# Rotary embedding: the early store of two rows replaced by an early write of 512 bytes of zeros per partition

## The chip, the cores and the metric

The kernel runs on one core of a Trainium2 chip. The metric is the device time in microseconds (us); lower is better. The kernel before took 317.1 us (median of 3 runs, 317.05 to 317.19).

A ratio below is the mean time of one kernel's runs over the mean of the other's runs of the same rounds, so it is not quite the ratio of the medians quoted beside it.

Some words first. HBM is the chip's large memory, SBUF the memory on the core, of 128 partitions. POOL (GpSimd), DVE (VectorE), ScalarE (ACT in the profile) and SyncE (SP) are engines of the core. POOL, ScalarE and SyncE each issue transfers to a queue of their own, and the same 16 DMA engines do the work of all queues. A transfer is a DMA; the trace has a record for each of its rows, called a packet here. When a DMA engine has done its part, it adds one to a counter, which is the completion increment, and also has a record; the DMA has landed when all 16 have come. An operation is gated by, or held behind, a DMA when it may start only after that has landed.

## The reference

`x` has shape (8, 2048, 16, 64) in float32. Each row of 64 is a pair of halves, rotated by an angle that depends on the position:

```python
x1, x2 = x[..., :32], x[..., 32:]
out1 = x1 * cos - x2 * sin
out2 = x1 * sin + x2 * cos
return np.concatenate([out1, out2], axis=-1)
```

67.1 MB are read and 67.1 MB written; there is little arithmetic.

## The kernel before

A batch is one tile: 128 partitions, each with 16 positions of 16 x 64 numbers, 64 KB in float32 in HBM and 32 KB in float16 in SBUF. The POOL queue loads with a cast to float16 and stores with a cast back. DVE does three operations per batch. There are five buffers, so five loads are issued at once, and later loads wait for stores to free a buffer.

The first two positions of batch 0 (`JA = 2`, 1 MB in all) go another way: they are loaded in float32 on the SyncE queue, worked on first, and written back on the SyncE queue by an early store, which is held behind load 3. In the code below, and in every diff, `...` marks what is left out.

```python
    def store(b, xt):
        j0 = JA if b == 0 else 0                 # batch 0: 14 of 16 positions
        nc.gpsimd.dma_start(out=..., in_=xt[:, j0:J, :, :]...)
    # ... rotate(xt, j0, j1): two multiplications and an addition on DVE ...
    tiles = [load(b) for b in range(NBUF)]       # NBUF = 5, POOL queue
    # ... ScalarE casts: head -> tiles[0], sin, -sin, cos ...
    rotate(tiles[0], 0, JA)
    nc.scalar.copy(out=head..., in_=tiles[0][:, 0:JA, :, :]...)
    early = nc.sync.dma_start(out=out[0]...[:, 0:JA, :]..., in_=head...)
    tc.add_manual_dep(early.ins, loads[3].ins.name, ...,
                      reason="the first rows go out behind this load")
    for b in range(B):
        rotate(tiles[b], JA if b == 0 else 0, J)
        if b < B - 1:
            store(b, tiles[b])
        if b + NBUF < B:
            tiles.append(load(b + NBUF))
    # ... the last batch goes out in three parts ...
```

Of the kernel before, what the change touches and what calls it, by code (L numbers as in the profile page):

```python
# [1 line left out]

# [4 lines left out]


@with_exitstack  # L10
def kernel(
    ctx: ExitStack,
    tc: tile.TileContext,
    x: bass.AP,
    cos: bass.AP,
    sin: bass.AP,
    out: bass.AP,
):
    nc = tc.nc
    f16 = mybir.dt.float16  # L20
    f32 = mybir.dt.float32

    B, S, H, D = x.shape
    Dh = D // 2
    P = nc.NUM_PARTITIONS
    J = S // P
    NBUF = 5

    const_pool = ctx.enter_context(tc.tile_pool(name="rope_const", bufs=1))
    io_pool = ctx.enter_context(tc.tile_pool(name="rope_io", bufs=NBUF))  # L30
    tmp_pool = ctx.enter_context(tc.tile_pool(name="rope_tmp", bufs=1))

    JA = 2
    head = const_pool.tile([P, JA, H, D], f32)
    x0 = x[0].rearrange("(p j) h d -> p j (h d)", j=J)
    nc.sync.dma_start(  # L36
        out=head.rearrange("p j h d -> p (j h d)"),
        in_=x0[:, 0:JA, :].rearrange("p j f -> p (j f)"),
    )
    sin_f = const_pool.tile([P, J, Dh], f32)  # L40
    cos_f = const_pool.tile([P, J, Dh], f32)
    cos_h = const_pool.tile([P, J, Dh], f16)
    sin_h = const_pool.tile([P, J, D], f16)
    nc.sync.dma_start(out=sin_f, in_=sin.rearrange("(p j) d -> p j d", j=J))  # L44
    nc.sync.dma_start(out=cos_f, in_=cos.rearrange("(p j) d -> p j d", j=J))

    loads = []

    def load(b):
        xt = io_pool.tile([P, J, H, D], f16)  # L50
        j0 = JA if b == 0 else 0
        dma = nc.gpsimd.dma_start(  # L52
            out=xt[:, j0:J, :, :].rearrange("p j h d -> p (j h d)"),
            in_=x[b].rearrange("(p j) h d -> p j (h d)", j=J)[:, j0:J, :].rearrange("p j f -> p (j f)"),
        )
        loads.append(dma)
        return xt

    def store(b, xt):
        j0 = JA if b == 0 else 0  # L60
        nc.gpsimd.dma_start(  # L61
            out=out[b].rearrange("(p j) h d -> p j (h d)", j=J)[:, j0:J, :].rearrange("p j f -> p (j f)"),
            in_=xt[:, j0:J, :, :].rearrange("p j h d -> p (j h d)"),
        )

    def rotate(xt, j0, j1):
        v = tmp_pool.tile([P, J, H, D], f16)
        n = j1 - j0
        js = slice(j0, j1)
        shape = [P, n, H, 2, Dh]  # L70
        sin_b = sin_h[:, js, :].rearrange("p j (e d) -> p j e d", e=2).unsqueeze(2).to_broadcast(shape)
        cos_b = cos_h[:, js, :].unsqueeze(2).to_broadcast([P, n, 2 * H, Dh])
        xe = xt[:, js, :, :].rearrange("p j h (e d) -> p j h e d", e=2)
        nc.vector.tensor_mul(  # L74
            out=v[:, js, :, :].rearrange("p j h (e d) -> p j h e d", e=2),
            in0=xe[:, :, :, ::-1, :],
            in1=sin_b,
        )
        xw = xt[:, js, :, :].rearrange("p j h (e d) -> p j (h e) d", d=Dh)
        nc.vector.tensor_mul(out=xw, in0=xw, in1=cos_b)  # L80
        xa = xt[:, js, :, :].rearrange("p j h d -> p (j h d)")
        nc.vector.tensor_add(out=xa, in0=xa, in1=v[:, js, :, :].rearrange("p j h d -> p (j h d)"))  # L82

    tiles = [load(b) for b in range(NBUF)]
    nc.scalar.copy(  # L85
        out=tiles[0][:, 0:JA, :, :].rearrange("p j h d -> p (j h d)"),
        in_=head.rearrange("p j h d -> p (j h d)"),
    )
    nc.scalar.copy(out=sin_h[:, :, Dh:D], in_=sin_f)  # L89
    nc.scalar.mul(out=sin_h[:, :, 0:Dh], in_=sin_f, mul=-1.0)  # L90
    nc.scalar.copy(out=cos_h, in_=cos_f)  # L91
    rotate(tiles[0], 0, JA)
    nc.scalar.copy(  # L93
        out=head.rearrange("p j h d -> p (j h d)"),
        in_=tiles[0][:, 0:JA, :, :].rearrange("p j h d -> p (j h d)"),
    )
    early = nc.sync.dma_start(
        out=out[0].rearrange("(p j) h d -> p j (h d)", j=J)[:, 0:JA, :].rearrange("p j f -> p (j f)"),
        in_=head.rearrange("p j h d -> p (j h d)"),
    )  # L100
    tc.add_manual_dep(
        early.ins,
        loads[3].ins.name,
        mybir.DependencyInfo(mybir.DependencyClass.Sync, mybir.DependencyReason.DATA),
        reason="the first rows go out behind this load",
    )
    def part(b, j0, j1):
        return (
            out[b].rearrange("(p j) h d -> p j (h d)", j=J)[:, j0:j1, :].rearrange("p j f -> p (j f)"),
            tiles[b][:, j0:j1, :, :].rearrange("p j h d -> p (j h d)"),  # L110
        )

    for b in range(B):
        rotate(tiles[b], JA if b == 0 else 0, J)
        if b < B - 1:
            store(b, tiles[b])
        if b + NBUF < B:
            tiles.append(load(b + NBUF))
    dst, src = part(B - 1, 0, 9)
    gate = nc.gpsimd.dma_start(out=dst, in_=src)  # L120
    dst, src = part(B - 1, 9, J - JA)
    rest = nc.gpsimd.dma_start(out=dst, in_=src)  # L122
    tc.add_manual_dep(
        rest.ins,
        gate.ins.name,
        mybir.DependencyInfo(mybir.DependencyClass.NoSync, mybir.DependencyReason.DATA),
        reason="order of the ring",
    )
    dst, src = part(B - 1, J - JA, J)
    nc.scalar.copy(out=head.rearrange("p j h d -> p (j h d)"), in_=src)  # L130
    end = nc.sync.dma_start(out=dst, in_=head.rearrange("p j h d -> p (j h d)"))
    tc.add_manual_dep(
        end.ins,
        gate.ins.name,
        mybir.DependencyInfo(mybir.DependencyClass.Sync, mybir.DependencyReason.DATA),
        reason="the last rows go out behind this part",
    )


# [1 line left out]
_INS = ['x', 'cos', 'sin']  # L141
_OUTS = [((8, 2048, 16, 64), 'float32')]


# [23 lines left out]
```

## Time and profile before

The first lines to read are those of the page: busy time, the DMA row in 40 slices (tenths of the 16 engines' time), the queues and the HBM traffic.

```profile
span 315.4 us, 127 instructions
...
DVE 209.1 (66%) x27; ACT 8.7 (3%) x7; POOL 9.4 (3%) x21
...
DMA  9899999999998989999999999999999999999998
...
q0 software_dynamic: 2448, 98.04, 97.2%
q1 hardware_dynamic: 720, 3.67, 7.7%
HBM read 67.63 MB, written 67.11 MB: 427 GB/s over the span
```

The DMA row never falls below 8: the DMA engines are the limit, and DVE at 66% is not. The two shares of the queues add up to over 100%: a few packet records are very long without moving data.

The second view is the timeline. Its columns are start, length, engine, line, operation, output and input, and in brackets how long the engine sat idle and what ended that. The length of a DMA line is only its issue.

```profile
34.09 1.23 DVE L80 TENSOR_TENSOR xt<-xt,cos_h 128x2048 f16<-128x2048 f16 x1 [17.13 <-ACT cos_h L91]
...
59.85 0.54 POOL L61 DMA_DIRECT2D out_dram<-xt  x1 [55.82 <-DVE xt L82]
...
81.74 0.35 SPq L97 DMA_DIRECT2D out_dram<-head  x1
...
86.03 0.54 POOL L61 DMA_DIRECT2D out_dram<-xt  x1 [25.64 <-DVE xt L82]
...
122.08 0.53 POOL L52 DMA_DIRECT2D xt<-in_x_dram  x1 [35.51 <-DMA out_dram<-xt]
...
141.19 0.53 POOL L52 DMA_DIRECT2D xt<-in_x_dram  x1 [18.58 <-DMA out_dram<-xt]
```

Stores 0 and 1 are issued at 60 and 86 us, but their data move only after load 4, which is ahead of them in the POOL queue. Load 5 waits for store 0 to land (122 us), load 6 for store 1 (141 us). The early store, line 97, is issued at 82 us. Its landing stands in the view of its line:

```profile
L97 SPq DMA_DIRECT2D out_dram<-head x1: 348/348/348, 81.7 to 81.7; - x1
...
DMA to landing us min/median/max: 39.6/39.6/39.6
```

It landed 39.6 us after its issue, near 121 us, although the packet records have its data through by about 106 us. The records also give the pace of each engine. This table is worked out from them; a "stage" here is the distance between the mean times at which the 16 engines write the completion increments of one DMA and of the one before it in the POOL queue.

| kernel before | us |
|---|---|
| one 64 KB row, load / store, on one engine | 2.432 / 2.449 |
| an ordinary load or store of 8 such rows per engine | 19.3 |
| stage of load 3 | 19.32 |
| stage of load 4 (the early store beside it) | 22.28 |
| stage of store 0 (14 positions of 16) | 17.22 |

Eight rows take 19.3 us and not 19.5 because the records of rows that follow one another overlap by some 0.02 to 0.04 us.

### The profile page before, as it was taken

The numbers are of one execution on the slowest core, as the hardware profiler recorded it, in microseconds if no ns is written. First come the engines' busy times: TensorE is split into PE (matmuls) and PEld (weight loads), VectorE is DVE, ScalarE is ACT, GpSimd is POOL, SyncE is SP. The second block draws the span as 40 slices with busy tenths as digits, with TensorE's granted clock in tenths as the row PEclk, the third lists the DMA queues.
The fourth block names the chain that finished last, engine by engine and source line by source line (L and its number), as shares of the span: only waits on it lengthen the run. The fifth ranks groups of instructions, "written<-read, shape, count | busy, mean of one in ns | idle before, by whom it ended". The sixth has DMA issues, their size and how long they took to land.

```text
span 315.4 us, 127 instructions
## 1 busy us (share of the span) xinstructions
DVE 209.1 (66%) x27; ACT 8.7 (3%) x7; POOL 9.4 (3%) x21
## 2 busy tenths in 40 slices
DVE  0010699999999999999999999994009994000000
ACT  4100300000000000000000000000000002000000
POOL 3000000000000000001000000100000001000000
DMA  9899999999998989999999999999999999999998
GB/s 279 184 261 207 199 233 233 199 199 258 222 224 191 501 364 501 399 332 262 204 199 199 399 399 399 424 507 266 199 258 474 399 399 515 416 399 399 432 432 333
DMA packets 3168, 101.71 MB, mean 322 GB/s; under 512 B 352, under 2 KB 352, under 8 KB 608
## 3 DMA queue, kind: packets, MB, share of 16 engines
q0 software_dynamic: 2448, 98.04, 97.2%
q1 hardware_dynamic: 720, 3.67, 7.7%
HBM read 67.63 MB, written 67.11 MB: 427 GB/s over the span
## 4 chain that ended last, share of the span: by engine, by line
DVE 25%; DMA 22%; issue 18%; another core or an unknown queue 17%; POOL 1%; ACT 1%; SPq 0%; POOLq 0%; ACTq 0%; DVEq 0%
DMA xt<-in_x_dram 12%; DMA cos_f<-in_cos_dram 10%; DVE xt L82 8%; DVE xt L80 8%; DVE v L74 8%; ACT head L130 1%; POOL out_dram L61 1%; POOL xt L52 0%; ACT cos_h L91 0%; SPq L44 0%; SPq L36 0%; POOLq L52 0%; POOLq L61 0%; ACTq L130 0%
## 5 line engine op out<-in xcount | busy, mean ns | idle before, releaser
L74 DVE TENSOR_TENSOR v<-xt,sin_h 128x16384 f16<-128x16384 f16 (+2 forms) x9 | 69.7, 7744 | 36.5 <-DMA xt<-in_x_dram 20.6
L80 DVE TENSOR_TENSOR xt<-xt,cos_h 128x16384 f16<-128x16384 f16 (+2 forms) x9 | 69.7, 7744 | 17.5 <-ACT cos_h L91 17.1
L82 DVE TENSOR_TENSOR xt<-xt,v 128x16384 f16<-128x16384 f16 (+2 forms) x9 | 69.7, 7744 | 0.3
L130 ACT CAST head<-xt 128x2048 f32<-128x2048 f16 x1 | 1.9, 1897 | 224.9 <-DVE xt L82 224.9
L52 POOL DMA_DIRECT2D xt<-in_x_dram x8 | 4.4, 560 | 111.0 <-DMA out_dram<-xt 110.2
L61 POOL DMA_DIRECT2D out_dram<-xt x7 | 3.7, 535 | 98.0 <-DVE xt L82 98.0
L85 ACT CAST xt<-head 128x2048 f16<-128x2048 f32 x1 | 1.9, 1897 | 3.4 <-DMA head<-in_x_dram 3.4
L93 ACT CAST head<-xt 128x2048 f32<-128x2048 f16 x1 | 1.9, 1901 | 2.6 <-DVE xt L82 2.6
L120 POOL DMA_DIRECT2D out_dram<-xt x1 | 0.5, 531 | 46.2 <-DVE xt L82 46.2
L85 ACT ACT_TABLE_LOAD x1 | 1.3, 1283 | 0.7 <-PEq L152 0.7
L91 ACT CAST cos_h<-cos_f 128x512 f16<-128x512 f32 x1 | 0.6, 617 | 17.7 <-DMA cos_f<-in_cos_dram 17.7
L89 ACT CAST sin_h<-sin_f 128x512 f16<-128x512 f32 x1 | 0.6, 617 | 7.2 <-DMA sin_f<-in_sin_dram 7.2
L90 ACT ACTIVATE sin_h<-sin_f 128x512 f16<-128x512 f32 x1 | 0.6, 624 | 0.0
L122 POOL DMA_DIRECT2D out_dram<-xt x1 | 0.5, 531 | 0.0
L152 POOL MEMSET const-float32-0.0<- 128x1 f32 x1 | 0.1, 98 | 0.2 <-issue 0.2
L152 POOL MEMSET const-bfloat16-1.0<- 128x1 bf16 x1 | 0.1, 101 | 0.0
L152 POOL MEMSET const-float32-1.0<- 128x1 f32 x1 | 0.1, 98 | 0.0
L152 POOL MEMSET const-uint8-127<- 128x1 uint8 x1 | 0.1, 98 | 0.0
## 6 DMA issues: line engine op xcount, KB each, us to landing
xt<-in_x_dram POOLq DMA_DIRECT2D x7, 4096.0 KB, 41.1
out_dram<-xt POOLq DMA_DIRECT2D x1, 7168.0 KB, 61.7
out_dram<-xt POOLq DMA_DIRECT2D x1, 4608.0 KB, 42.4
xt<-in_x_dram POOLq DMA_DIRECT2D x1, 3584.0 KB, 22.3
out_dram<-xt POOLq DMA_DIRECT2D x1, 2560.0 KB, 47.9
out_dram<-head SPq DMA_DIRECT2D x2, 1024.0 KB, 24.0
head<-in_x_dram SPq DMA_DIRECT2D x1, 1024.0 KB, 4.7
sin_f<-in_sin_dram SPq DMA_DIRECT2D x1, 256.0 KB, 13.4
```

Source lines behind the costliest of these rows:

```text
L52: dma = nc.gpsimd.dma_start(out=xt[:, j0:J, :, :].rearrange("p j h d -> p (j h d)"), in_=x[b].rearrange("(p j) h d -> p j (h d)", j=J)[:, ...
L61: nc.gpsimd.dma_start(out=out[b].rearrange("(p j) h d -> p j (h d)", j=J)[:, j0:J, :].rearrange("p j f -> p (j f)"), in_=xt[:, j0:J, :, :] ...
L74: nc.vector.tensor_mul(out=v[:, js, :, :].rearrange("p j h (e d) -> p j h e d", e=2), in0=xe[:, :, :, ::-1, :], in1=sin_b,)
L80: nc.vector.tensor_mul(out=xw, in0=xw, in1=cos_b)
L82: nc.vector.tensor_add(out=xa, in0=xa, in1=v[:, js, :, :].rearrange("p j h d -> p (j h d)"))
L85: nc.scalar.copy(out=tiles[0][:, 0:JA, :, :].rearrange("p j h d -> p (j h d)"), in_=head.rearrange("p j h d -> p (j h d)"),)
L89: nc.scalar.copy(out=sin_h[:, :, Dh:D], in_=sin_f)
L90: nc.scalar.mul(out=sin_h[:, :, 0:Dh], in_=sin_f, mul=-1.0)
L91: nc.scalar.copy(out=cos_h, in_=cos_f)
L93: nc.scalar.copy(out=head.rearrange("p j h d -> p (j h d)"), in_=tiles[0][:, 0:JA, :, :].rearrange("p j h d -> p (j h d)"),)
L120: gate = nc.gpsimd.dma_start(out=dst, in_=src)
L130: nc.scalar.copy(out=head.rearrange("p j h d -> p (j h d)"), in_=src)
```

## The change

The early store goes, and with it the splitting of batch 0 on DVE and in store 0. In its place a tile of zeros is written to the first 512 bytes of each partition's rows of batch 0, from the ScalarE queue, once load 2 has landed. Store 0 overwrites the zeros, so the result is the same. The intent that can be read from the diff is to keep "a first write" early, but a sixteenth of its size and ahead of the need. The early load of two positions on the SyncE queue stays.

```diff
     def store(b, xt):
-        j0 = JA if b == 0 else 0
         nc.gpsimd.dma_start(
-            out=out[b]...[:, j0:J, :]..., in_=xt[:, j0:J, :, :]...,
+            out=out[b].rearrange("(p j) h d -> p j (h d)", j=J), in_=xt
         )
 # ... rotate() likewise takes the whole tile ...
-    rotate(tiles[0], 0, JA)
-    nc.scalar.copy(out=head..., in_=tiles[0][:, 0:JA, :, :]...)
-    early = nc.sync.dma_start(out=out[0]...[:, 0:JA, :]..., in_=head...)
+    zero = const_pool.tile([P, 128], f32)
+    nc.gpsimd.memset(zero, 0.0)
+    blank = nc.scalar.dma_start(
+        out=out[0].rearrange("(p j) h d -> p j (h d)", j=J)[:, 0, 0:128], in_=zero
+    )
     tc.add_manual_dep(
-        early.ins,
-        loads[3].ins.name,
+        blank.ins,
+        loads[2].ins.name,
         ...
-        reason="the first rows go out behind this load",
+        reason="a first write behind this load",
     )
 ...
-        rotate(tiles[b], JA if b == 0 else 0, J)
+        rotate(tiles[b])
```

More of the change, by code (lines that the diff above doesn't have):

```diff
@@ L59, in store, with rotate @@
     def store(b, xt):
-        j0 = JA if b == 0 else 0
         nc.gpsimd.dma_start(
-            out=out[b].rearrange("(p j) h d -> p j (h d)", j=J)[:, j0:J, :].rearrange("p j f -> p (j f)"),
-            in_=xt[:, j0:J, :, :].rearrange("p j h d -> p (j h d)"),
+            out=out[b].rearrange("(p j) h d -> p (j h d)", j=J), in_=xt
         )
-    def rotate(xt, j0, j1):
+    def rotate(xt):
         v = tmp_pool.tile([P, J, H, D], f16)
-        n = j1 - j0
-        js = slice(j0, j1)
-        shape = [P, n, H, 2, Dh]
-        sin_b = sin_h[:, js, :].rearrange("p j (e d) -> p j e d", e=2).unsqueeze(2).to_broadcast(shape)
-        cos_b = cos_h[:, js, :].unsqueeze(2).to_broadcast([P, n, 2 * H, Dh])
-        xe = xt[:, js, :, :].rearrange("p j h (e d) -> p j h e d", e=2)
+        shape = [P, J, H, 2, Dh]
+        sin_b = sin_h.rearrange("p j (e d) -> p j e d", e=2).unsqueeze(2).to_broadcast(shape)
+        cos_b = cos_h.unsqueeze(2).to_broadcast([P, J, 2 * H, Dh])
+        xe = xt.rearrange("p j h (e d) -> p j h e d", e=2)
         nc.vector.tensor_mul(
-            out=v[:, js, :, :].rearrange("p j h (e d) -> p j h e d", e=2),
-            in0=xe[:, :, :, ::-1, :],
-            in1=sin_b,
+            out=v.rearrange("p j h (e d) -> p j h e d", e=2), in0=xe[:, :, :, ::-1, :], in1=sin_b
         )
-        xw = xt[:, js, :, :].rearrange("p j h (e d) -> p j (h e) d", d=Dh)
+        xw = xt.rearrange("p j h (e d) -> p j (h e) d", d=Dh)
         nc.vector.tensor_mul(out=xw, in0=xw, in1=cos_b)
-        xa = xt[:, js, :, :].rearrange("p j h d -> p (j h d)")
-        nc.vector.tensor_add(out=xa, in0=xa, in1=v[:, js, :, :].rearrange("p j h d -> p (j h d)"))
+        xa = xt.rearrange("p j h d -> p (j h d)")
+        nc.vector.tensor_add(out=xa, in0=xa, in1=v.rearrange("p j h d -> p (j h d)"))
     tiles = [load(b) for b in range(NBUF)]
@@ L91 @@
     nc.scalar.copy(out=cos_h, in_=cos_f)
-    rotate(tiles[0], 0, JA)
-    nc.scalar.copy(
-        out=head.rearrange("p j h d -> p (j h d)"),
-        in_=tiles[0][:, 0:JA, :, :].rearrange("p j h d -> p (j h d)"),
-    )
-    early = nc.sync.dma_start(
-        out=out[0].rearrange("(p j) h d -> p j (h d)", j=J)[:, 0:JA, :].rearrange("p j f -> p (j f)"),
-        in_=head.rearrange("p j h d -> p (j h d)"),
+    zero = const_pool.tile([P, 128], f32)
+    nc.gpsimd.memset(zero, 0.0)
+    blank = nc.scalar.dma_start(
+        out=out[0].rearrange("(p j) h d -> p j (h d)", j=J)[:, 0, 0:128], in_=zero
     )
     tc.add_manual_dep(
-        early.ins,
-        loads[3].ins.name,
+        blank.ins,
+        loads[2].ins.name,
         mybir.DependencyInfo(mybir.DependencyClass.Sync, mybir.DependencyReason.DATA),
-        reason="the first rows go out behind this load",
+        reason="a first write behind this load",
     )
```

## The prediction

> **What bounds the kernel.** The DMA engines. The page's DMA row reads 8 or 9 in all 40 slices; the packet records run from 1.8 us to 314 us of the 315.4 us span. In them one 64 KB row costs one engine 2.432 us as a load and 2.449 us as a store, about 27 GB/s, or 430 GB/s for 16. Eight batches of eight such rows per engine, both ways, are 8 x 19.46 + 8 x 19.59 = 312.4 us. The Trainium skill ("DMA: Bandwidth & Descriptors", section Bandwidth) gives 425 GB/s measured for one core; the trace agrees (427 GB/s of HBM traffic over the span). DVE is busy only 66%. The chain of waits names DVE and "issue" often, but no DMA engine is idle meanwhile.
>
> **What the change does.**
> - The bytes of batch 0 stay: 1 MB leaves the SyncE queue, and store 0 grows from 7 to 8 MB. In the records the 1 MB stretched load 4 from the usual 19.3 us to 22.4 us (+3.0), while store 0 took 17.2 us, not 19.3 (-2.1): these rows cost 0.9 us more as 8 KB packets beside another queue than as part of long rows. That is saved.
> - Added: 128 rows of 512 bytes, 8 per engine. The 2 KB packets of sine and cosine take 0.084 to 0.096 us; my estimate for the small ones is 0.03 to 0.1 us each, 0.2 to 0.8 us in all.
> - One ACT cast of 1.9 us goes, three small DVE operations merge into large ones, a POOL memset comes. DVE finishes batch 0 near 52 us rather than 59.6: it multiplies by sine when load 0 lands (24 us) and waits for cosine until 34. Off the critical path: stores 0 and 1 stand behind load 4 in the POOL queue until about 101 us anyway.
>
> **The one new dependency.** Store 0 overwrites the zeros, so it waits on POOL until they have landed, and so do all DMAs issued behind it. Load 2 lands at 62 us. The Trainium skill (same page, section Queues, rings and completion order) says that an engine takes turns between queues packet by packet; the trace agrees: cosine's 8 packets per engine were spread over 19 us, the early store's came every 2.7 us. So the zeros need 20 to 24 us and land near 84 to 86 us, some 15 us before the loads run out. Nothing starves. The risk: the early store's completion increments were held 12.7 to 14.8 us, until store 0 was through (landing 39.6 us after issue). If the zeros' increments are held until load 4 is through, store 0 is issued near 102 us and the engines idle 2 to 3 us.
>
> **Sum.** 317.1 - 0.9 + 0.4 = 316.6 us; with held increments about 320. Store 0's rows run at the usual rate from the first, so I see no start-up penalty for "a first write" to hide. Predicted 316.6 us, range 315.8 to 319.5. Faster by over 2%: 0.01; within 2%: 0.94; slower by over 2%: 0.05.
>
> **What would show it.** Right: DMA row still 8s and 9s; load 4's increments near 101 us instead of 103.7; stores 0 and 1 through near 120 and 139.7; the zeros landing 20 to 25 us after issue; batch 0 done on DVE near 52 us. Wrong: a slice under 8 near 100 us, or store 0 issued on POOL after 100 us (held increments); rows over 2.45 us in the store stages; engines ending at different times.
>
> **What would make it wrong.** Increments held longer than thought; a slow state after the 512-byte writes; the early megabyte hiding a cost at the first change from reading to writing that this trace can't show.

## The result

The changed kernel took 317.40 us (median of 6 runs, 317.34 to 317.62) beside 317.09 us (6 runs, 317.04 to 317.19). The ratio is 1.001, with a 95% interval of 0.9998 to 1.0023. So it is the same within 2%, inside the stated range, and 0.8 us above the predicted point. The sign of the small difference was predicted wrongly: 0.5 us faster was expected, 0.3 us slower came.

The page after:

```profile
span 315.8 us, 123 instructions
...
DVE 208.6 (66%) x24; ACT 6.8 (2%) x6; POOL 9.6 (3%) x22
...
DMA  9899999999999999999999999999999999999997
...
q0 software_dynamic: 2448, 99.09, 97.9%
q1 hardware_dynamic: 576, 2.62, 2.2%
q10 hardware_dynamic: 144, 0.07, 0.1%
HBM read 67.63 MB, written 67.17 MB: 427 GB/s over the span
```

The engines are as full as before (the last slice, in which the work ends, reads 7 and not 8). The timeline after, for the operations that answer to those shown:

```profile
36.43 8.69 DVE L74 TENSOR_TENSOR xt<-xt,cos_h 128x16384 f16<-128x16384 f16 x1 [3.88 <-ACT cos_h L85]
45.15 8.69 DVE L76 TENSOR_TENSOR xt<-xt,v 128x16384 f16<-128x16384 f16 x1
...
62.67 0.37 ACTq L88 DMA_DIRECT2D out_dram<-zero  x1
...
87.04 1.07 POOL L60 DMA_DIRECT2D out_dram<-xt  x2 [82.79 <-DMA out_dram<-zero]
...
122.03 0.54 POOL L52 DMA_DIRECT2D xt<-in_x_dram  x1 [33.92 <-DMA out_dram<-xt]
...
141.60 0.54 POOL L52 DMA_DIRECT2D xt<-in_x_dram  x1 [19.03 <-DMA out_dram<-xt]
```

And the landing of the zeros, in the view of the DMA issues (KB, us from issue to landing):

```profile
out_dram<-zero ACTq DMA_DIRECT2D x1, 64.0 KB, 23.8
```

Store 0 is now issued at 87 us and not at 60, because POOL waits for the zeros; and yet load 5, which waits for store 0 to land, is issued at 122.03 us against 122.08. The 27 us were slack, as the prediction said. The stages, from the packet records as before:

| stage, us | before | changed |
|---|---|---|
| load 3 | 19.32 | 19.57 |
| load 4 | 22.28 | 20.32 |
| store 0 | 17.22 | 19.30 |
| sum of the three | 58.82 | 59.19 |
| mean of load 4's last 16 rows (one per engine) | 3.02 | 3.42 |

From the end of store 0 on, all stages agree within 0.02 us in the two traces. So the difference, 0.37 us, lies in these three. The zeros add 0.25 us to load 3. The surprise is in load 4: it moves nothing but its own rows and a last few of the zeros, and still takes 1.0 us more than the 19.32 us of an ordinary load. The last row shows where. Each engine's last row of load 4, just ahead of its first store row, lasts 3.42 us in the records in place of 2.43. I call this the stretch. The same rows last 3.02 us in the kernel before, and I had overlooked them. At the later changes from loads to stores neither trace has any such row.

The stretch can be seen in the DMA view of the changed kernel from 96 to 112 us. It has 40 slices of 0.4 us, and the bytes of a row stand in the slice in which the row starts:

```profile
GB/s 492 0 0 0 0 737 573 0 0 0 0 0 0 655 1475 492 0 0 0 655 1475 492 0 0 0 492 1638 492 0 0 0 328 1802 492 0 0 0 328 1802 492
```

The last load rows start near 98.4 us, in the sixth and seventh slice, and the first store rows over three microseconds later, in slices 14 to 16. From there on the rows follow every six slices.

### The profile page after: what moved, and what is told of

Same layout as the page of the kernel before. It is cut to its first block, busy times and chain, and to the rows that moved or that the text cites. A ratio compares the mean times of both kernels' runs of the same rounds, so it can differ in the third digit from the quotient of the medians.

```text
span 315.8 us, 123 instructions
## 1 busy us (share of the span) xinstructions
DVE 208.6 (66%) x24; ACT 6.8 (2%) x6; POOL 9.6 (3%) x22
## 4 chain that ended last, share of the span: by engine, by line
DMA 41%; issue 24%; another core or an unknown queue 8%; DVE 8%; ACT 1%; POOL 1%; SPq 0%; POOLq 0%; ACTq 0%; DVEq 0%
DMA xt<-in_x_dram 12%; DMA out_dram<-xt 11%; DMA cos_f<-in_cos_dram 11%; DMA out_dram<-zero 8%; DVE v L70 3%; DVE xt L74 3%; DVE xt L76 3%; ACT head L120 1%; POOL xt L52 0%; POOL out_dram L60 0%; ACT cos_h L85 0%; SPq L44 0%; SPq L36 0%; POOLq L60 0%
## 5 line engine op out<-in xcount | busy, mean ns | idle before, releaser
L70 DVE TENSOR_TENSOR v<-xt,sin_h 128x16384 f16<-128x16384 f16 x8 | 69.5, 8692 | 50.8 <-DMA xt<-in_x_dram 50.6
L74 DVE TENSOR_TENSOR xt<-xt,cos_h 128x16384 f16<-128x16384 f16 x8 | 69.5, 8692 | 4.1 <-ACT cos_h L85 3.9
L76 DVE TENSOR_TENSOR xt<-xt,v 128x16384 f16<-128x16384 f16 x8 | 69.5, 8692 | 0.3
L120 ACT CAST head<-xt 128x2048 f32<-128x2048 f16 x1 | 1.9, 1897 | 227.5 <-DVE xt L76 227.5
```

The source lines that it names most:

```text
L70: nc.vector.tensor_mul(out=v.rearrange("p j h (e d) -> p j h e d", e=2), in0=xe[:, :, :, ::-1, :], in1=sin_b)
L74: nc.vector.tensor_mul(out=xw, in0=xw, in1=cos_b)
L76: nc.vector.tensor_add(out=xa, in0=xa, in1=v.rearrange("p j h d -> p (j h d)"))
L120: nc.scalar.copy(out=head.rearrange("p j h d -> p (j h d)"), in_=src)
```

## The experiments

My theory after reading the two traces (theory A): the DMA engines limit both kernels; the zeros cost their packets and buy nothing; store 0's new wait has about 15 us of slack; and the saving that I had expected was eaten by the stretch. Rivals: the zeros hide some of the cost of the first stores; the wait costs something; the earlier end of batch 0 on DVE is worth something. Twelve runs were made, on three chips. On these the kernel before took 317.19, 317.13 and 317.23 us (medians of 9 runs each). Each quoted passage is the expectation before the run. The stages of one kernel repeat to about 0.1 us from trace to trace: the sum of the three is 59.19 and 59.15 us for the changed kernel, 58.95 and 58.86 us with no early write (runs 1 and 11). The stretch itself varies more: load 4's last rows took 3.20 to 3.48 us in the traces of runs 1, 3 and 7 to 12. The kernel before has one trace.

### 1. No early write at all

```diff
-    zero = const_pool.tile([P, 128], f32)
-    nc.gpsimd.memset(zero, 0.0)
-    blank = nc.scalar.dma_start(...)
-    tc.add_manual_dep(blank.ins, loads[2].ins.name, ...)
```

> The changed kernel without the write of zeros and its memset: no early write at all. Theory A (an early write as such buys nothing; the zeros cost their packets and store 0's wait has slack): 0.2 to 0.5 us faster than the changed kernel, 316.9 to 317.2 us, level with the kernel before, and the last round of load 4's rows, just ahead of the first store, again takes 3.0 to 3.8 us a row in place of 2.43. Rival B (the zeros hide part of a start-up cost of the first stores): slower than the changed kernel by 0.5 us or more, with those rows, or store 0's first ones, longer still.

Measured: 317.29 us (5 runs, 317.17 to 317.45), ratio to the kernel before 1.000 (0.9987 to 1.0013). The stage of load 3 is 19.33 us: the 0.25 us of the zeros is gone. Load 4 takes 20.32 us, and its last rows 3.41 us, as with the zeros. So 512 bytes per partition hide nothing. The time is 0.11 us below the changed kernel's 317.40 us, less than the 0.2 to 0.5 us expected and just outside 316.9 to 317.2 us; run 11 compares the two on one chip. POOL's timeline is worth a look:

```profile
52.06 0.54 POOL L60 DMA_DIRECT2D out_dram<-xt  x1 [48.02 <-DVE xt L76]
77.97 0.54 POOL L60 DMA_DIRECT2D out_dram<-xt  x1 [25.37 <-DVE xt L76]
121.70 0.53 POOL L52 DMA_DIRECT2D xt<-in_x_dram  x1 [43.19 <-DMA out_dram<-xt]
```

Store 0 is issued at 52 us here, at 60 us in the kernel before, at 87 us in the changed one, and the load behind it at 121.7, 122.1 and 122.0 us. The time of issue does not matter while the queue is full.

### 2. The zeros one load later

```diff
-        loads[2].ins.name,
+        loads[3].ins.name,
```

> The changed kernel with the zeros gated by load 3 and not load 2. Theory A (the change is harmless only because the zeros land some 15 us before the loads run out, and store 0 on POOL waits for them): the zeros are issued near 82 us, their eighth packets come as the loads end, they land at 102 to 105 us, store 0 is issued about half a microsecond later, and the 16 engines idle 2.5 to 6 us near 102 to 108: 319.5 to 323.5 us. Rival B (store 0's wait is not on the critical path at all): within 0.5 us of the changed kernel.

Measured: 319.21 us (4 runs, 319.11 to 319.32), ratio 1.006 (1.0046 to 1.0074). The DMA row of the page and POOL's and ScalarE's timelines:

```profile
DMA  9899999999996999999999999999999999999998
```

```profile
102.50 1.07 POOL L60 DMA_DIRECT2D out_dram<-xt  x2 [98.25 <-DMA out_dram<-zero]
123.77 0.53 POOL L52 DMA_DIRECT2D xt<-in_x_dram  x1 [20.20 <-DMA out_dram<-xt]
```

```profile
82.19 0.37 ACTq L88 DMA_DIRECT2D out_dram<-zero  x1
```

A slice of 6 appears where both kernels have a 9. Now POOL's wait ends after the loads do: store 0 is issued at 102.5 us, its first rows start at 103.6 us, and an engine stands without a row for 2.8 us on average. This shows that the wait is real and that only the gate behind load 2 gives it slack. The miss in my expectation (319.5 us at the least) has a reason in the records: load 4's last rows took 2.45 us here. With no store queued behind them there was no stretch (whether a like cost was hidden in the idle time is not shown), so the net loss was 61.03 - 59.19 = 1.84 us over the three stages, and the time is 1.8 us above the 317.40 us of the changed kernel (which was measured in another call).

### 3. The zeros one load later, in the rows of batch 7

```diff
-        out=out[0]...[:, 0, 0:128], in_=zero
+        out=out[B - 1]...[:, 0, 0:128], in_=zero
...
-        loads[2].ins.name,
+        loads[3].ins.name,
```

> As the run behind load 3, but the zeros go to the rows of batch 7, whose stores come last, so store 0 doesn't wait for them. Theory A (it is the wait for the landing, not the writing of zeros at this place, that costs): within 0.4 us of the changed kernel, 317.0 to 317.8 us, no idle near 102 us. Rival B (a small write beside the first store disturbs the engines): 319 us or more, with idle or long rows near 102 us. On held increments: if increments behind a write to HBM are held while stores run on the other queue, those of these zeros are held too, 10 us or longer, and they land near 121 us.

Measured: 317.52 us (4 runs, 317.46 to 317.90), ratio 1.0006 (0.9991 to 1.0022). The loss of run 2 is gone though the write happens at the same time: it was the wait, not the write. The zeros now take longer to land:

```profile
out_dram<-zero ACTq DMA_DIRECT2D x1, 64.0 KB, 40.0
```

Their increments lasted 14.5 to 16.9 us in the records and all ended by 121.7 us, with store 0. This is what the early store's increments did in the kernel before (12.7 to 14.8 us). The zeros of the changed kernel, whose increments came while loads ran, had increments of 0.02 us. So the held increment that I had named as the risk is real, and goes with stores running on the other queue.

### 4. The early megabyte one load earlier

The kernel before, with one word changed:

```diff
-        loads[3].ins.name,
+        loads[2].ins.name,
```

> The kernel before with its early megabyte gated by load 2 and not load 3, so that it is through by about 86 us, well ahead of the first store. Theory A (the first store on the POOL queue has a start-up cost of about 0.9 us per engine whatever was written before, and the early megabyte only overlapped it): the last round of load 4's rows takes 3.3 to 3.8 us as in the changed kernel, and the time is 0.2 to 0.6 us above the kernel before. Rival B (any megabyte written early warms the path for writes): those rows take 2.8 us or less and the time is at most that of the kernel before.

Measured: 317.06 us (5 runs, 317.03 to 317.39), ratio 0.9995 (0.9982 to 1.0007). Theory A fell here: load 4's last rows took 2.50 us, as the rival said, and the time is not above the kernel before (the 0.13 us below it is within the scatter). An early megabyte takes the stretch away from load 4's last rows even when its data are through some 17 us before the first store; in the kernel before it did so by less than half (3.02 us). But it has its own price. Load 3 took 22.10 us and load 4 19.70, store 0 16.89: 2.78 + 0.38 - 2.41 = 0.75 us more than if the two positions had gone with the long rows, against 1.0 us of stretch. The three stages add up to 58.69 us against 58.95 with no early write and 58.82 in the kernel before.

Most of that price is again in load rows, which I had overlooked. The records show load 3's rows beside the megabyte longer than 2.43 us, by 0.56 us per engine in all, of which 0.26 us in the last row. So the megabyte moved more than half of the lengthening from load 4 to load 3. Counted over both loads it is 0.98 us with no early write, 0.76 us in the kernel before and 0.63 us here; only about 0.1 us is then left as the price of the small packets.

### 5 and 6. A megabyte of zeros, to batch 0 and to batch 7

To see what in the early megabyte counts, the changed kernel was given 8 KB of zeros per partition; the first buffer, `head`, cleared after its use, is the source.

```diff
-    zero = const_pool.tile([P, 128], f32)
+    zero = head.rearrange("p j h d -> p (j h d)")
...
-        out=out[0]...[:, 0, 0:128], in_=zero
+        out=out[0]...[:, 0:2, :].rearrange("p j f -> p (j f)"), in_=zero      # run 6: out[B - 1]
```

> The changed kernel with 8 KB of zeros per partition (the first buffer, cleared after its use, as the source) in place of 512 bytes, same queue, same gate, same batch. Theory A (what takes away the stretch of load 4's last rows before the first store is the amount written early, not the queue or the real data): those rows take 2.4 to 2.7 us, as with the early megabyte behind load 2, and the megabyte costs about 22.1 - 19.3 = 2.8 us in load 3 and 0.4 us in load 4: 319.0 to 319.6 us. Rival B (it is the SyncE queue, or that store 0 is a row shorter): the rows take 3.2 to 3.8 us as in the changed kernel, and the time is 319.9 to 320.6 us.

> The same 8 KB of zeros per partition, but to the rows of batch 7, which store 0 doesn't touch. Theory A (only the amount counts, not the place written): as the run with 8 KB to batch 0, load 4's last rows at 2.4 to 2.7 us and the time within 0.4 us of it. Rival B (it is the place: store 0 is quick to start where its own rows have been written before): load 4's last rows take 3.2 to 3.8 us again.

Measured: load 4's last rows took 2.61 us (batch 0) and 2.44 us (batch 7). The DMA view of the second, from 96 to 112 us as above, has rows every six slices, with no gap before the first store rows in slices 19 to 22:

```profile
GB/s 983 82 82 164 0 0 983 82 82 164 0 0 901 164 82 164 0 0 1638 492 164 328 0 0 1638 492 164 328 0 0 1638 492 164 328 0 0 1638 492 164 328
```

So, by one trace each, it takes neither the SyncE queue, nor real data, nor a write to store 0's own rows to free load 4's last rows of the stretch. Here too load 3's rows were longer instead, by 0.48 and 0.63 us per engine in all; over both loads it is 0.66 and 0.63 us. The three stages add up to 61.13 and 61.11 us, 1.9 us above the changed kernel, as expected. The times missed the expectation: 320.68 us (4 runs, 319.84 to 321.73; ratio 1.0122, 1.0102 to 1.0142) and 320.48 us (4 runs, 320.06 to 321.05; ratio 1.0106, 1.0092 to 1.0119). The traced run of the first is its fastest, 319.84 us. What the slower, untraced runs lost beyond that stays open.

### 7. A small store in the POOL queue itself

No early write from ScalarE, but 512 bytes per partition, cast from float16, between load 3 and load 4 in the POOL queue, to batch 7:

```diff
+    zero = const_pool.tile([P, 128], f16)
+    nc.gpsimd.memset(zero, 0.0)
-    tiles = [load(b) for b in range(NBUF)]
+    tiles = [load(b) for b in range(NBUF - 1)]
+    nc.gpsimd.dma_start(out=out[B - 1]...[:, 0, 0:128], in_=zero)
+    tiles.append(load(NBUF - 1))
```

> The kernel with no early write, plus a small store of zeros (512 bytes per partition in float32, cast from float16, to batch 7) in the POOL queue itself, between load 3 and load 4. Theory A (the stretch belongs to the first store of the POOL queue, whatever its size): about 1 us extra appears at the end of load 3 near 81 us, load 4's last rows take 2.43 us, and the time is 317.2 to 317.8 us. Rival B (it takes a large early write to use it up): load 4's last rows take 3.2 to 3.8 us and nothing over 0.4 us appears near 81 us; the time is in the same range, so the rows decide, not the time.

Measured: 317.76 us (4 runs, 317.59 to 317.87), ratio 1.0018 (1.0004 to 1.0032). Load 3 and the small store together took 0.26 us more than a load alone, and load 4's last rows still lasted 3.48 us. So the stretch does not belong to the first store of the POOL queue whatever its size: the rival was right.

### 8. DVE later by one operation

```diff
... # rotate() gets a second argument: if it is true, the multiplication by sine is done twice
-        rotate(tiles[b])
+        rotate(tiles[b], b == 0)
```

> The changed kernel, with the first multiplication of batch 0 done twice on DVE (8.7 us more), so that batch 0 is done near 59 us as in the kernel before and not near 54. Theory A (DVE is off the critical path, and the earlier end of batch 0 is worth nothing): within 0.2 us of the changed kernel, 317.2 to 317.6 us. Rival B (the earlier end of batch 0 is worth something that the other terms hide): slower by 0.5 us or more.

Measured: 318.04 us (5 runs, 317.60 to 318.40), ratio 1.0027 (1.0014 to 1.0039). This is 0.6 us above the changed kernel's 317.40 us, which was measured in another call, and taken alone it is what rival B said (0.5 us or more). Its trace spoke for theory A: from the mean increment of load 0 to that of the last POOL store it takes 288.85 us, the changed kernel 288.87. What was longer was the distance of the slowest DMA engine from the mean of the 16: 0.9 us at the last POOL store, 0.3 us in the changed kernel. At load 0, before 24 us and ahead of the edited operation, it was already 0.8 us (0.4 us in the changed kernel). So it was run again beside the changed kernel.

### 9, 10 and 11. The changed kernel, run 8 and run 1 again, on one chip

> The changed kernel unaltered, for a comparison on the same chip as the next two. All theories: 317.3 to 317.7 us; the mean increment of load 0 to that of the last store on the POOL queue 288.8 to 288.9 us apart, as in its first trace.

> The run with one DVE multiplication of batch 0 done twice, again, because it came out 0.6 us above the changed kernel of another chip although its trace shows the same work of the engines after load 0. Theory A (DVE is off the critical path; the 0.6 us was chip and start-up scatter, one engine late before 24 us, ahead of the edit): within 0.25 us of the changed kernel beside it. Rival B (the later end of batch 0 costs something): 0.4 us or more above it.

> The kernel with no early write, again, beside the changed kernel on one chip. Theory A (the zeros cost their packets, 0.25 us, and buy nothing): 0.1 to 0.4 us below the changed kernel. Rival B (they buy something): level with it or above.

| 5 runs each | median us | lowest to highest | ratio to before (95%) |
|---|---|---|---|
| changed kernel | 317.58 | 317.29 to 317.63 | 1.0007 (0.9994 to 1.0021) |
| with DVE later | 317.72 | 317.32 to 318.14 | 1.0014 (1.0001 to 1.0026) |
| no early write | 317.47 | 317.25 to 317.54 | 1.0004 (0.9992 to 1.0017) |

DVE later costs 0.14 us by the medians, within the scatter. From the mean increment of load 0 to that of the last POOL store its trace takes 288.59 us, and the changed kernel's 288.81. That is theory A: the earlier end of batch 0 is worth nothing that these runs resolve. The 0.6 us of run 8 did not come again in the median, though in this trace too the slowest DMA engine is 0.8 us behind the mean, at load 0 and at the end. The kernel with no early write is 0.11 us below the changed kernel by the medians, in the direction of theory A and at the edge of what these runs resolve; in the traces the stage of load 3 is 19.33 and 19.32 us without the zeros and 19.57 us with them, both times.

### 12. 2 KB of zeros per partition

```diff
-        out=out[0]...[:, 0, 0:128], in_=zero
+        out=out[0]...[:, 0, 0:512], in_=zero[:, 0:512]      # zero is head, cleared
```

> The changed kernel with 2 KB of zeros per partition. 512 bytes left the stretch of load 4's last rows at 3.4 us, 8 KB took it to 2.4 to 2.6 us. Theory A (the amount written early decides, by degrees): those rows take 2.7 to 3.3 us. Rival B (the row has to be long, or the packets 8 KB): 3.3 to 3.6 us as with 512 bytes. Rival C (2 KB are already enough): 2.4 to 2.6 us.

Measured, in a single run of 318.19 us: load 4's last rows took 3.34 us. The changed kernel itself had 3.36 us on that chip. So 2 KB do not take the stretch away from these rows and 8 KB do. Where between them it goes, and whether by the size of a packet or of the whole, was not tried.

## Why the prediction was right, and where a term was off

**Right: the bound and the class.** Nearly every slice of the DMA row is full before and after, and the change moves almost the same bytes. The Trainium skill ("Perfetto Trace Analysis", section Identifying the Most-Contended Engine) advises judging DMA by HBM utilization rather than by occupancy. Here the two agree: 427 GB/s of HBM traffic in both traces, beside the 430 GB/s that 16 engines would reach at the pace of the rows in the records.

**Right: the new dependency has slack.** The zeros were predicted to land 20 to 25 us after issue, at 84 to 86 us; they landed after 23.8 us, at 86.5 us. Their packets came one per engine every 2.45 us, one load row apart, so 64 KB took as long as a load of 8 MB and somewhat more. With each record taken as a packet, this agrees with the Trainium skill ("DMA: Bandwidth & Descriptors", section Queues, rings and completion order), by which an engine goes round its queues packet by packet. Run 2 shows the other side: with the same write one load later the wait costs 1.8 us.

**Right: DVE and the time of issue don't count.** Batch 0 was done at 53.8 us (52 predicted; cosine landed 2.3 us later in this trace). Runs 8 and 10 moved it to about 59 us; run 1 issued store 0 at 52 us. None moved the stages behind.

**Right: the zeros' own cost.** 0.25 us in load 3, against 0.2 to 0.8 predicted. One 512-byte packet took 0.040 us in the records.

**Off: "these rows cost 0.9 us more as 8 KB packets beside another queue than as part of long rows. That is saved."** This was the step that failed, and with it "Store 0's rows run at the usual rate from the first, so I see no start-up penalty". Store 0's rows did run at the usual rate; the cost stood just ahead of them, in load 4's last rows, which I had not looked at. Of the 0.9 us (0.86 by the stages: 2.96 more in load 4, 2.10 less in store 0), 3.02 - 2.43 = 0.59 us was the stretch before the first store. About 0.2 us more stood in the first rows of load 4, beside the early packets, and only about 0.1 us is left as the price of the small packets. The changed kernel saves the 0.1 and the 0.2 us but pays the stretch in full, 3.42 - 2.43 = 0.99 us. So the term is -0.1 - 0.2 - 0.6 + 1.0 = +0.1 us in place of -0.9; with +0.25 us for the zeros that makes about 0.35 us, beside 0.37 us in the stages and 0.31 us in the medians. The increments of load 4 came at 101.5 to 102.0 us for the same reason, and not near 101. The prediction did name, as what would make it wrong, a cost at the first change from reading to writing that the early megabyte hides; it said that the trace can't show it, but the rows of 3.02 us were there to be seen.

**Partly luck: the range.** A term that was off by 1.0 us stayed inside a range of 3.7 us, the upper part of which allowed for another risk, the held increments. No term of the sum reaches 0.4% of the time, so a forecast of "the same" was safe whatever became of the stretch.

**What an early write buys.** Small ones (512 bytes and 2 KB per partition) bought nothing. Early megabytes took most of the stretch from load 4's last rows, but more than half of what they took came back in the rows of load 3: counted over both loads, the engines lost 0.63 to 0.66 us each in runs 4 to 6, against 0.98 us with no early write. With the small packets' own price run 4 gains 0.26 us in the three stages. No version tried is better than the kernel before by more than the scatter; the lowest median is that of run 4, 317.06 us, with an interval of the ratio that holds 1.

**What stays open.** Why the last load rows ahead of the first large stores take 1 us longer, once and not at later changes, is not settled, and neither is why rows of load 3 are longer beside an early megabyte. The runs show that a small first store of the POOL queue does not use it up (run 7), that it does not go with the rows written (runs 5 and 6), and that it is not there where no store is queued behind the loads (run 2).

## What to carry to other kernels

Here, with all DMA engines full and transfers queued up behind one another, the issue of a store moved by 35 us (52 to 87 us), and the end of a batch on DVE by 5, with no effect on the time that these runs could resolve; what counted was the packets each engine had to carry and whether a wait outlasted the queue. A small transfer beside a full queue took one row of the other queue, 2.45 us, per packet, so whatever waits for it needs that much slack: gate it a whole load earlier than seems necessary, or let nothing wait for it. And when a stage is costed from a trace, look at the last packets before a change from loads to stores as well as the first ones after it.

## What the Trainium skill lacked or had wrong

- "DMA: Bandwidth & Descriptors", Anatomy of one DMA: the fit of 2.0 us plus bytes over 436 GB/s would give 2.15 us for 64 KB (an estimate from that page, whose fit is for DMAs issued from POOL). The zeros, issued from ScalarE beside a full POOL queue, took 23.8 us. So the page isn't shown to be wrong; it has the rule of the turns, but no time for a small DMA beside a busy queue: here, 8 packets per engine at 2.45 us each, plus about 4 us.
- The same page, Queues, rings and completion order, says that an increment lands only after every earlier write of its engine. Here increments behind a write to HBM were held 12.7 to 16.9 us, past store rows that began after them on the other queue, until that whole store was through (kernel before and run 3); beside loads they took 0.02 us (changed kernel and run 4). The page does not tell the two cases apart.
- No page has the stretch: the last load row of each engine before the first large stores of the kernel took 3.2 to 3.5 us in place of 2.43, once; an earlier write of 8 KB per partition took it to 2.4 to 2.6 us but lengthened the load rows beside it by about 0.5 to 0.6 us per engine, 2 KB did not.
